# Hybrid encoder kernel: low halves on VectorE, first head's values split out of PSUM, late operands and attention loads placed elsewhere

## The chip, the cores and the metric

The kernel runs on one core of a Trainium2 chip. The metric is device time in microseconds of one launch. Engines are named as in the profile: PE (TensorE) multiplies, DVE (VectorE), ACT (ScalarE) and POOL (GpSimd) work on tiles in on-chip memory (SBUF) and in the accumulator banks (PSUM), SP starts most of the DMA transfers. Every engine runs its instructions in one fixed order and stands still at an instruction whose inputs or whose output's memory isn't ready.

## The reference

Two layers over 1024 tokens of 1024 features, float32 throughout. Layer 0 is a retention mixer with 4 heads (keys of 256, values of 512), layer 1 attends in chunks with 16 heads of 64; each is followed by a squared-ReLU MLP of width 4096.

```python
proj = h @ w_in                                   # retention: q | k | v | g
q = _rope(q, pos);  k = _rope(k, pos) * DK ** -0.5
scores  = einsum(q, k) * intra_decay;  o = scores @ v + (q @ state) * query_decay
o = (o - mean) * rsqrt(var + EPS) * gn_g          # per head
y = (silu(g) * o) @ w_out
...
s = q @ k.T * scale + bias;  p = softmax(s);  y = (p @ v) @ w_out      # attention, band of 576 keys
...
u = relu(h @ w1);  y = (u * u) @ w2               # MLP
x = x + y                                          # after each, with an RMSNorm in front
```

## The kernel before

**Products.** Every large product is three matmuls (`mm3`, L161 to L166): operand and weight are each split into a high half, rounded to TensorE's fast type, and a low half, the rest; high x high, low x high and high x low are summed in PSUM. `split` (L132) makes the halves: the high one as a cast on ACT (L136), the low one as a subtraction on DVE or, where `lo_eng` says "pool", on POOL (L140). So L136 and L140 appear in the profile for many tiles, told apart by their names: vh/vl values of retention, yh/yl its gated output, oh/ol attention's output, whi/wlo weights, ptl transposed probabilities, xl operands of the MLP.

**Stages, by time in the profiled execution.** Projections of q and k with rope (50 to 330 us), of the values (to 440) and of the gate (to 556); retention core, one head after the other (556 to 900); MLP up (to 1240) and down (to 1600); attention's q, k and v (to 1850); attention core (1855 to 2118); MLP up and down again (to the end).

**Values of retention.** `proj_tok` (L451) computes one head's values for 8 token tiles in 8 PSUM banks, and `evac` scales each on ACT and stores it to a DRAM buffer vS. In the core, `issue` (L752) loads q, k and v pieces into a ring of 4 `raw` tiles and `take` (L766) splits them: q and k with DVE, v with ACT and POOL; then it issues the next load, whose ring slot is free when that split has ended. `turn_k` transposes the keys (kth, ktl at L793), `score` (L804) makes the scores, which are masked with maskt (L811) and split (sh, sl). The heads' outputs are normalized by a chain of small operations on tiles of 128x2 (`sm`, L850 to L858, with the square root of L852 on ACT), which ends in `on` (L862, ACT), is transposed by PE (L884), multiplied by the gate (yt, L886) and split (yh, yl).

**Sevens.** Large square products go by seven products of sums instead of eight (`Seven`, L353). `go` runs the products in the order of `steps`: of the first two groups products 1, 2, 5 and 6, then (0,3), (1,3), (0,7), (0,4), (1,7), (1,4), then group by group. `ready` prepares weights two steps ahead: `sums` (L334) adds weight blocks into wS tiles, of which 3 can live at once, and `make` splits them into wh and wl. The operands of products 3, 7 and 4 are made by twelve `late` steps (L301), four for each: t, xh and xl for product 3 (L313), then t3 and its split, then t4 (L319, L320) and its split. `spread` (L426) hangs them behind the products; the scheduler then places them among the rest of each engine's order. The norm's last part (`turn`) hangs behind product 4.

**Attention core.** For each of 16 heads and 4 row groups, `scores` puts q times k into PSUM (pS), DVE adds the bias (bt), writes pr and a row statistic into `sm` (L1144), ACT exponentiates (L1148), DVE inverts the sum (L1149), POOL scales pr (L1150), PE transposes (pt, L1168), ACT and DVE split it (pth, ptl), PE multiplies by the values (po, L1180), ACT and DVE add up osum (L1187, L1188), and osum is split (oh on ACT, ol on POOL). `att_out` multiplies finished heads by the output weights in between; its wlo are on POOL for the heads within the core. `load_q`, `load_k` and `load_b` issue the loads of a head on SP.

Of the kernel before, what the change touches and what calls it, by code (L numbers as in the profile page):

```python
# [9 lines left out]
F32 = mybir.dt.float32  # L10
F32R = mybir.dt.float32r
# [5 lines left out]
P = 128  # L17
S = 1024
# [58 lines left out]
def trunk_kernel(ctx: ExitStack, tc: tile.TileContext, I, out):  # L77
# [246 lines left out]
    class Group:  # L324
# [9 lines left out]
        def sums(self, ws, products):  # L334
            a = self.a
            for p in products:
                self.s[p] = t = ws.tile([P, 4, P], F32, name="wS", tag="wS", bufs=3)
                if p == 5:
                    nc.vector.tensor_tensor(out=t, in0=a[1, 0], in1=a[1, 1], op=ALU.add)
                elif p == 6:  # L340
                    nc.vector.tensor_tensor(out=t, in0=self.s[5], in1=a[0, 0], op=ALU.subtract)
                elif p == 7:
                    nc.vector.tensor_tensor(out=t, in0=a[1, 0], in1=a[0, 0], op=ALU.subtract)
                else:
                    nc.vector.tensor_tensor(out=t, in0=a[0, 1], in1=self.s[6], op=ALU.subtract)
# [80 lines left out]
    def spread(norm, xb, psp, more=()):  # L426

        gen = norm.late(xb)
        hooks = {s: [] for s in range(12)}
        for hf in range(2):  # L430
            hooks[2].append(lambda hf=hf: norm.sums(psp, hf))
            hooks[Seven.NORM].append(lambda hf=hf: norm.turn(psp, hf))
        for i in range(12):
            hooks[1 + (i * 3) // 4].append(lambda: next(gen))
        for s, f in more:
            hooks.setdefault(s, []).append(f)
        return hooks
# [164 lines left out]
    with ExitStack() as ph:  # L602
# [92 lines left out]
        vsc = gp.tile([P, NB, RH], F32, name="vsc")  # L695
        for i in range(RH):
            nc.vector.tensor_tensor(out=vsc[:, :, i], in0=vdec[:, :, i], in1=rcol, op=ALU.mult)
        for hd in range(RH):
            def evac(t, ps, hd=hd):
                vt = tmp_tile(gp, "t")  # L700
                nc.scalar.activation(vt, ps, AF.Copy, scale=vsc[:, t, hd:hd + 1])
                DMA.dma_start(out=vS[hd][t * P:(t + 1) * P, :], in_=vt)
            proj_tok(psp, norm, w_in[:, 2 * D + hd * DV:2 * D + (hd + 1) * DV], evac)

        yp = pool(rs, "yR", RIGHT)
        cq = pool(rq, "coreRqk", RIGHT)
        qk, vv, kt, sc, stt = {}, {}, {}, {}, {}

        def qk_tiles():
            return [cq.tile([P, 2, HT], F32R, name=n, tag=n, bufs=3) for n in ("qkh", "qkl")]  # L710
# [21 lines left out]
    with ExitStack() as ph:  # L732
# [6 lines left out]
        with ExitStack() as st:  # L739
            cp = pool(st, "coreR", RIGHT)  # L740
            pa = pool(st, "psR", None, 8, PSUM)
            maskt = cp.tile([P, RH, P], F32, name="maskt")
            nc.scalar.dma_start(out=maskt, in_=I["mask"])
            fill = Filler()


            items = [(hd, hf, what) for hd in range(RH) for hf in range(2) for what in ("q", "k", "v0", "v1")]
            items = [it for it in items if it not in ((0, 0, "q"), (0, 0, "k"))]
            raws, issued = {}, [0]
            RING = 4  # L750

# [14 lines left out]
            def take(hd, hf, what):  # L766
                if hd == RH:
                    return
                raw = raws[hd, hf, what]
                if what in "qk":  # L770
                    hi, lo = qk[hd, what, hf] = qk_tiles()
                    split(raw, hi, lo)
                else:
                    hi, lo = (cp.tile([P, 2, DV], F32R, name=n, tag=n, bufs=3) for n in ("vh", "vl"))
                    split(raw, hi, lo, "act", "pool")
                    for x in range(2):
                        vv[hd, hf * 4 + 2 * int(what[1]) + x] = (hi[:, x, :], lo[:, x, :])
                if (what, hf) != ("k", 0):
                    issue()
# [96 lines left out]
            def gate(hd, hf, pr, res):  # L876
                ons, gt = res, gtile[hd, hf, pr]
                if pr == 0:
                    ybuf[hd, hf] = tuple(yp.tile([P, 4, HT], F32R, name=n, tag=n, bufs=2) for n in ("yh", "yl"))
                yh, yl = ybuf[hd, hf]  # L880
                for z in range(2):
                    pt = pa.tile([P, 4, P], F32, name="pt", tag="ps")
                    for e in range(4):
                        nc.tensor.transpose(pt[:, e, :], ons[z][:, e * P:(e + 1) * P], ident)  # L884
                    yt = cp.tile([P, 4, P], F32, name="yt", tag="yt", bufs=2)
                    nc.vector.tensor_tensor(out=yt, in0=pt, in1=gt[:, :, z * P:(z + 1) * P], op=ALU.mult)  # L886
                    tsl = slice((2 * pr + z) * P, (2 * pr + z + 1) * P)
                    split(yt, yh[:, :, tsl], yl[:, :, tsl], "act", "pool")
                load_gate()

            for _ in range(RING):
# [4 lines left out]
            for hd in range(RH):  # L896
                if late is not None:
                    fill.gens.append(tail)
                for J in range(4):
                    score(hd, 0, J)  # L900
                take(hd, 0, "v0")
                take(hd, 0, "v1")
                turn_k(hd)
                if late is not None:
                    fill.step(2)
                    gate(*late)
                state(hd, 0)
                state(hd, 1)
                fill.step(4)
                take(hd, 1, "q")  # L910
                take(hd, 1, "k")
                fill.step(3)
                ra = outs(hd, 0, 0)
                fill.step(2)
                rb = outs(hd, 0, 1)
                fill.drain()
                box = dict(psp=pa)
                tail = out_proj(box, hd)
                next(tail)
                gate(hd, 0, 0, ra)  # L920
                for J in range(4):
                    score(hd, 1, J)
                take(hd, 1, "v0")
                take(hd, 1, "v1")
                gate(hd, 0, 1, rb)
                ra = outs(hd, 1, 0)
                if hd + 1 < RH:
                    take(hd + 1, 0, "q")
                rb = outs(hd, 1, 1)
                if hd + 1 < RH:  # L930
                    take(hd + 1, 0, "k")
                gate(hd, 1, 0, ra)
                late = (hd, 1, 1, rb)
# [119 lines left out]
    with ExitStack() as ph:  # L1053
# [9 lines left out]
            DMA.dma_start(out=T[hd, "q"].bitcast(F32), in_=qA[hd // 2][hd % 2].rearrange("z f c -> (z f) c"))  # L1063

        def load_k(hd):
            t = cq.tile([P, 2, S], F32R, name="kk", tag="kk", bufs=2)
            src = kA[hd // 2][hd % 2]
            for z in range(2):
                DMA.dma_start(out=t[z * DH:(z + 1) * DH].bitcast(F32), in_=src)
# [9 lines left out]
            nc.gpsimd.memset(bt[DH:P, 0:DH], -NEG)  # L1079
            T[hd, "b"] = bt  # L1080

        for hd in range(2):
            load_q(hd)
            load_k(hd)
            load_b(hd)

        obuf = {}

# [4 lines left out]
        with ExitStack() as st:  # L1093
# [77 lines left out]
            def values(hd, g):  # L1171
# [16 lines left out]
                nc.vector.tensor_tensor(out=osum[mine, :], in0=po[mine, :], in1=osum[mine, :], op=ALU.add)  # L1188
                sl = slice(g * 2 * P, (g + 1) * 2 * P)
                oh, ol = obuf[p]  # L1190
                split(osum[mine, :], oh[mine, sl], ol[mine, sl], "act", "pool")

            units = [(hd, g) for hd in range(AH) for g in (0, 2, 1, 3)]
            n = len(units)
# [4 lines left out]
            for i in range(n + L2):  # L1199
# [8 lines left out]
                if i >= L2:  # L1208
                    values(*units[i - L2])
                    j = i - L2 + 1  # L1210
                    if j in (16, 32):
                        fill.add(att_out(dict(psp=pF), j // 8 - 2, 2, "pool"))
                if L1 <= i < n + L1:
                    turn(*units[i - L1], 2)
                fill.step(1)
# [96 lines left out]
```

## Time and profile before

| | us |
|---|---|
| median of 3 runs | 2859.15 (2856.14 to 2859.59) |
| profiled execution, its own time | 2858.98 |
| its span | 2857.2 |
| PE busy | 2763.7 (97%) |
| DVE busy | 1624.3 (57%) |
| ACT busy | 1080.7 (38%) |
| POOL busy | 305.1 (11%) |

The span is one execution as the hardware profiler saw it; the own time of that execution is 1.8 us longer. PE is busy nearly all the time, so the views that count are those that show where it waits, at which clock it runs, and what ends its waits. The mean granted clock is 0.985 of full speed; a share of 0.50 in a stretch is the lower of the clock's two levels, 1.2 of 2.4 GHz.

### The profile page before, as it was taken

The numbers are of one execution on the slowest core, as the hardware profiler recorded it, in microseconds if no ns is written. First come the engines' busy times: TensorE is split into PE (matmuls) and PEld (weight loads), VectorE is DVE, ScalarE is ACT, GpSimd is POOL, SyncE is SP. The second block draws the span as 40 slices with busy tenths as digits, with TensorE's granted clock in tenths as the row PEclk, the third lists the DMA queues.
The fourth block names the chain that finished last, engine by engine and source line by source line (L and its number), as shares of the span: only waits on it lengthen the run. The fifth ranks groups of instructions, "written<-read, shape, count | busy, mean of one in ns | idle before, by whom it ended". The sixth has DMA issues, their size and how long they took to land.

```text
span 2857.2 us, 34484 instructions
## 1 busy us (share of the span) xinstructions
PE 2763.7 (97%) x12762; PEld 2272.0 (80%) x12762; DVE 1624.3 (57%) x2851; ACT 1080.7 (38%) x1932; POOL 305.1 (11%) x351
## 2 busy tenths in 40 slices
PE   8999999989999999999999899989999999999998
PEld 7888888768877788878888778769877888788887
DVE  5431123366557766654545877678878666544545
ACT  4001221243225544432213534478875444422222
POOL 1320000042111000000000000255540000000000
PEclk9999999989999999999999999999999999999999
DMA  4322333342211332343322265685621333433321
GB/s 142 107 91 78 107 114 99 114 155 93 84 52 37 103 111 100 115 141 106 108 77 85 55 201 153 166 211 143 169 71 51 116 115 111 140 100 103 111 85 59
DMA packets 247770, 313.02 MB, mean 110 GB/s; under 512 B 14665, under 2 KB 172465, under 8 KB 245553
## 3 DMA queue, kind: packets, MB, share of 16 engines
q1 hardware_dynamic: 245792, 306.30, 34.8%
q0 software_dynamic: 1536, 4.20, 0.5%
q8 instruction: 100, 1.64, 0.3%
q14 instruction: 70, 0.57, 0.1%
q10 hardware_dynamic: 272, 0.32, 0.0%
HBM read 222.64 MB, written 90.74 MB: 110 GB/s over the span
## 4 chain that ended last, share of the span: by engine, by line
PE 86%; DVE 6%; ACT 4%; issue 2%; DMA 1%; POOL 0%; SPq 0%; POOLq 0%; DVEq 0%; ACTq 0%
PE ps L165 18%; PE ps L164 18%; PE ps L166 18%; PE pA L164 6%; PE pA L166 5%; PE pA L165 5%; PE pC L164 3%; PE pC L166 3%; PE pC L165 3%; PE pB L164 1%; PE pB L166 1%; PE pB L165 1%; PE po L1180 1%; PE pt L1168 1%; ACT pr L1148 1%
## 5 line engine op out<-in xcount | busy, mean ns | idle before, releaser
L491 DVE TENSOR_TENSOR h<-ps,h 128x512 f32<-128x512 f32 x352 | 242.2, 689 | 343.3 <-PE ps L166 342.3
L136 ACT CAST whi<-wraw 128x1024 fp32r<-128x1024 f32 x132 | 139.0, 1053 | 765.2 <-PE ps L165 580.6
L165 PE MATMUL ps<-ul,whi 128*128 128x512 f32 x960 | 374.0, 390 | 1.8 <-DVE ul L140 1.8
L166 PE MATMUL ps<-uh,wlo 128*128 128x512 f32 x960 | 373.5, 389 | 0.0
L164 PE MATMUL ps<-uh,whi 128*128 128x512 f32 x960 | 373.1, 389 | 0.0
L164 PE MATMUL pA<-xh,wh 128*128 128x512 f32 x704 | 279.1, 401 | 12.3 <-ACT wh L136 9.3
L166 PE MATMUL pA<-xh,wl 128*128 128x512 f32 x704 | 277.4, 395 | 8.5 <-DVE wl L140 8.5
L165 PE MATMUL pA<-xl,wh 128*128 128x512 f32 x704 | 278.4, 395 | 0.0
L140 DVE TENSOR_TENSOR wlo<-wraw,whi 128x1024 fp32r<-128x1024 f32 x127 | 160.1, 1260 | 173.1 <-ACT whi L136 173.0
L165 PEld LDWEIGHTS ps<-ul,whi 128*128 128x128 f32 x960 | 180.2, 188 | 41.1 <-DVE ul L140 3.6
L164 PEld LDWEIGHTS ps<-uh,whi 128*128 128x128 f32 x960 | 180.0, 188 | 38.1 <-ACT uh L136 0.9
L166 PEld LDWEIGHTS ps<-uh,wlo 128*128 128x128 f32 x960 | 180.2, 188 | 37.1
L164 PE MATMUL ps<-hhi,whi 128*128 128x512 f32 x512 | 202.8, 396 | 2.3 <-ACT whi L136 1.5
L165 PE MATMUL ps<-hlo,whi 128*128 128x512 f32 x512 | 202.3, 395 | 0.0
L166 PE MATMUL ps<-hhi,wlo 128*128 128x512 f32 x512 | 202.3, 395 | 0.0
L164 PEld LDWEIGHTS pA<-xh,wh 128*128 128x128 f32 x704 | 134.3, 191 | 51.8 <-DVE c L417 13.4
L166 PEld LDWEIGHTS pA<-xh,wl 128*128 128x128 f32 x704 | 133.6, 190 | 38.9 <-DVE wl L140 10.1
L165 PEld LDWEIGHTS pA<-xl,wh 128*128 128x128 f32 x704 | 134.2, 191 | 27.4
L136 ACT CAST wh<-wS 128x512 fp32r<-128x512 f32 x176 | 109.1, 621 | 120.4 <-PE pB L165 57.4
L164 PE MATMUL pC<-xh,wh 128*128 128x512 f32 x352 | 139.8, 397 | 2.3 <-ACT wh L136 2.3
L166 PE MATMUL pC<-xh,wl 128*128 128x512 f32 x352 | 140.4, 399 | 0.6 <-DVE wl L140 0.6
L140 DVE TENSOR_TENSOR wl<-wS,wh 128x512 fp32r<-128x512 f32 x176 | 120.9, 687 | 33.6 <-ACT wh L136 33.0
(229 smaller groups left out, 5660.4 us busy)
## 6 DMA issues: line engine op xcount, KB each, us to landing
wr<-in_mlp_w_dram SPq DMA_DIRECT2D x32, 1024.0 KB, 5.5
uD<-c SPq DMA_DIRECT2D x128, 256.0 KB, 2.0
wraw<-in_mlp_w_dram SPq DMA_DIRECT2D x64, 512.0 KB, 3.5
xr<-uD SPq DMA_DIRECT2D x128, 256.0 KB, 3.1
wraw<-in_ret_w_in_dram SPq DMA_DIRECT2D x48, 512.0 KB, 4.1
kk<-kA SPq DMA_DIRECT2D x32, 512.0 KB, 8.4
wr<-in_att_w_in_dram SPq DMA_DIRECT2D x12, 1024.0 KB, 5.2
vS<-t SPq DMA_DIRECT2D x32, 256.0 KB, 2.0
```

Of the source, the lines that this page charges most:

```text
L136: nc.scalar.copy(out=hi, in_=src)
L140: eng.tensor_tensor(out=lo, in0=src, in1=hi.bitcast(F32), op=ALU.subtract)
L164: nc.tensor.matmul(ps, lhsT=lh, rhs=rh, start=start, stop=False, skip_group_check=more)
L165: nc.tensor.matmul(ps, lhsT=lh, rhs=rl, start=False, stop=False, skip_group_check=more)
L166: nc.tensor.matmul(ps, lhsT=ll, rhs=rh, start=False, stop=stop, skip_group_check=more)
L491: nc.vector.tensor_tensor(out=hv, in0=ps, in1=hv, op=ALU.add)
L1148: nc.scalar.activation(pr[:, :w], pr[:, :w], AF.Exp, bias=sm[:, 0:1], scale=-1.0, accum_out=sm[:, 1:2])
L1168: nc.tensor.transpose(pt[:, c - done:c - done + P], pr[:, (kb - k0) * P:(kb - k0 + 1) * P], ident)
L1180: nc.tensor.matmul(po[:, oc:oc + n], lhsT=T[hd, "v"][:, kb, :], rhs=t[:, off[kb]:off[kb] + n], start=i == 0, stop=i == len(seq) - 1)
```

## The change

Six edits. (1) `sums` may hold four wS tiles. (2) The twelve `late` steps hang behind products 0, 0, 1, 1, 2, 3, 4, 4, 5, 6, 7, 8 in place of 1, 1, 2, 3, 4, 4, 5, 6, 7, 7, 8, 9. (3) The first half of head 0's values (t < 4) is split straight from PSUM in `evac`, the high half by ACT, the low half by one operation of DVE, into tiles that the pool yR offers for retention's output later; those pieces are no longer stored, loaded or taken. (4) The mask is loaded by SP into a pool opened earlier, not by ACT's queue at the core's start. (5) The low halves vl (14 left, 128x1024), yl (32, 128x512), ol (64, 64x256) and the core's four wlo (128x1024) are made by DVE, not POOL. (6) The keys of even and odd heads have a tile of their own each, and the loads before attention go out as k0, q0, q1, b0, k1, b1; the first key tile thereby gets the memory that q's tile had before, and q's the keys'.

```diff
--- before.py
+++ after.py
@@ -334,7 +334,7 @@
         def sums(self, ws, products):
             a = self.a
             for p in products:
-                self.s[p] = t = ws.tile([P, 4, P], F32, name="wS", tag="wS", bufs=3)
+                self.s[p] = t = ws.tile([P, 4, P], F32, name="wS", tag="wS", bufs=4)
                 if p == 5:
                     nc.vector.tensor_tensor(out=t, in0=a[1, 0], in1=a[1, 1], op=ALU.add)
                 elif p == 6:
@@ -431,7 +431,7 @@
             hooks[2].append(lambda hf=hf: norm.sums(psp, hf))
             hooks[Seven.NORM].append(lambda hf=hf: norm.turn(psp, hf))
         for i in range(12):
-            hooks[1 + (i * 3) // 4].append(lambda: next(gen))
+            hooks[(0, 0, 1, 1, 2, 3, 4, 4, 5, 6, 7, 8)[i]].append(lambda: next(gen))
         for s, f in more:
             hooks.setdefault(s, []).append(f)
         return hooks
@@ -695,16 +695,26 @@
         vsc = gp.tile([P, NB, RH], F32, name="vsc")
         for i in range(RH):
             nc.vector.tensor_tensor(out=vsc[:, :, i], in0=vdec[:, :, i], in1=rcol, op=ALU.mult)
+        yp = pool(rs, "yR", RIGHT)
+        vv = {}
+        v0 = [yp.tile([P, 4, HT], F32R, name=n, tag=n, bufs=2) for n in ("yh", "yl")]
         for hd in range(RH):
             def evac(t, ps, hd=hd):
+                if hd == 0 and t < 4:
+                    hi, lo = vv[0, t] = tuple(z[:, t, :] for z in v0)
+                    sc = vsc[:, t, 0:1]
+                    nc.scalar.activation(hi, ps, AF.Copy, scale=sc)
+                    nc.vector.scalar_tensor_tensor(out=lo, in0=ps, scalar=sc, in1=hi.bitcast(F32), op0=ALU.mult, op1=ALU.subtract)
+                    return
                 vt = tmp_tile(gp, "t")
                 nc.scalar.activation(vt, ps, AF.Copy, scale=vsc[:, t, hd:hd + 1])
                 DMA.dma_start(out=vS[hd][t * P:(t + 1) * P, :], in_=vt)
             proj_tok(psp, norm, w_in[:, 2 * D + hd * DV:2 * D + (hd + 1) * DV], evac)
 
-        yp = pool(rs, "yR", RIGHT)
         cq = pool(rq, "coreRqk", RIGHT)
-        qk, vv, kt, sc, stt = {}, {}, {}, {}, {}
+        qk, kt, sc, stt = {}, {}, {}, {}
+        maskt = cq.tile([P, RH, P], F32, name="maskt")
+        DMA.dma_start(out=maskt, in_=I["mask"])
 
         def qk_tiles():
             return [cq.tile([P, 2, HT], F32R, name=n, tag=n, bufs=3) for n in ("qkh", "qkl")]
@@ -739,13 +749,11 @@
         with ExitStack() as st:
             cp = pool(st, "coreR", RIGHT)
             pa = pool(st, "psR", None, 8, PSUM)
-            maskt = cp.tile([P, RH, P], F32, name="maskt")
-            nc.scalar.dma_start(out=maskt, in_=I["mask"])
             fill = Filler()
 
 
             items = [(hd, hf, what) for hd in range(RH) for hf in range(2) for what in ("q", "k", "v0", "v1")]
-            items = [it for it in items if it not in ((0, 0, "q"), (0, 0, "k"))]
+            items = [it for it in items if it[:2] != (0, 0)]
             raws, issued = {}, [0]
             RING = 4
 
@@ -772,7 +780,7 @@
                     split(raw, hi, lo)
                 else:
                     hi, lo = (cp.tile([P, 2, DV], F32R, name=n, tag=n, bufs=3) for n in ("vh", "vl"))
-                    split(raw, hi, lo, "act", "pool")
+                    split(raw, hi, lo)
                     for x in range(2):
                         vv[hd, hf * 4 + 2 * int(what[1]) + x] = (hi[:, x, :], lo[:, x, :])
                 if (what, hf) != ("k", 0):
@@ -885,7 +893,7 @@
                     yt = cp.tile([P, 4, P], F32, name="yt", tag="yt", bufs=2)
                     nc.vector.tensor_tensor(out=yt, in0=pt, in1=gt[:, :, z * P:(z + 1) * P], op=ALU.mult)
                     tsl = slice((2 * pr + z) * P, (2 * pr + z + 1) * P)
-                    split(yt, yh[:, :, tsl], yl[:, :, tsl], "act", "pool")
+                    split(yt, yh[:, :, tsl], yl[:, :, tsl])
                 load_gate()
 
             for _ in range(RING):
@@ -898,8 +906,9 @@
                     fill.gens.append(tail)
                 for J in range(4):
                     score(hd, 0, J)
-                take(hd, 0, "v0")
-                take(hd, 0, "v1")
+                if hd:
+                    take(hd, 0, "v0")
+                    take(hd, 0, "v1")
                 turn_k(hd)
                 if late is not None:
                     fill.step(2)
@@ -1063,7 +1072,7 @@
             DMA.dma_start(out=T[hd, "q"].bitcast(F32), in_=qA[hd // 2][hd % 2].rearrange("z f c -> (z f) c"))
 
         def load_k(hd):
-            t = cq.tile([P, 2, S], F32R, name="kk", tag="kk", bufs=2)
+            t = cq.tile([P, 2, S], F32R, name="kk", tag=f"kk{hd % 2}", bufs=1)
             src = kA[hd // 2][hd % 2]
             for z in range(2):
                 DMA.dma_start(out=t[z * DH:(z + 1) * DH].bitcast(F32), in_=src)
@@ -1079,10 +1088,8 @@
             nc.gpsimd.memset(bt[DH:P, 0:DH], -NEG)
             T[hd, "b"] = bt
 
-        for hd in range(2):
-            load_q(hd)
-            load_k(hd)
-            load_b(hd)
+        for f, hd in ((load_k, 0), (load_q, 0), (load_q, 1), (load_b, 0), (load_k, 1), (load_b, 1)):
+            f(hd)
 
         obuf = {}
 
@@ -1188,7 +1195,7 @@
                 nc.vector.tensor_tensor(out=osum[mine, :], in0=po[mine, :], in1=osum[mine, :], op=ALU.add)
                 sl = slice(g * 2 * P, (g + 1) * 2 * P)
                 oh, ol = obuf[p]
-                split(osum[mine, :], oh[mine, sl], ol[mine, sl], "act", "pool")
+                split(osum[mine, :], oh[mine, sl], ol[mine, sl])
 
             units = [(hd, g) for hd in range(AH) for g in (0, 2, 1, 3)]
             n = len(units)
@@ -1209,7 +1216,7 @@
                     values(*units[i - L2])
                     j = i - L2 + 1
                     if j in (16, 32):
-                        fill.add(att_out(dict(psp=pF), j // 8 - 2, 2, "pool"))
+                        fill.add(att_out(dict(psp=pF), j // 8 - 2, 2))
                 if L1 <= i < n + L1:
                     turn(*units[i - L1], 2)
                 fill.step(1)
```

On DVE in the first Seven, at the change from the weights of products 1, 2, 5 and 6 to those of 3, 7 and 4 (wl and wS are weights, t and xl operands, c results). Before, the sum wS(1,7) of L343 and its wl stand late:

```order
L319 SCALAR_TENSOR_TENSOR t_6844<-h_86,gall,xh_6219 128x512
L140 TENSOR_TENSOR xl_6609<-t_6821,xh_6608 128x512
L320 TENSOR_TENSOR t_6844<-t_6844,xl_6220 128x512
L535 SCALAR_TENSOR_TENSOR c<-c,rB 128x512
L343 TENSOR_TENSOR wS<-wr 128x512
L140 TENSOR_TENSOR xl_6609<-t_6844,xh_6608 128x512
L140 TENSOR_TENSOR wl<-wr,wh 128x512
L417 TENSOR_TENSOR c<-pC,s_6814 128x512
L319 SCALAR_TENSOR_TENSOR t_6872<-h_88,gall,xh_6219 128x512
L535 SCALAR_TENSOR_TENSOR c<-c,rB 128x512
L320 TENSOR_TENSOR t_6872<-t_6872,xl_6220 128x512
L140 TENSOR_TENSOR wl<-wS,wh 128x512
```

With the change the first late operands and both sums of L343 stand ahead of the first L535:

```order
L140 TENSOR_TENSOR wl<-wS,wh 128x512
L140 TENSOR_TENSOR xl_6574<-t_6650,xh_6573 128x512
L345 TENSOR_TENSOR wS<-wr,wS 128x512
L313 SCALAR_TENSOR_TENSOR t_6674<-h_83,gall,b_6673 128x512
L343 TENSOR_TENSOR wS<-wr 128x512
L140 TENSOR_TENSOR wl<-wS,wh 128x512
L140 TENSOR_TENSOR xl_6574<-t_6674,xh_6573 128x512
L343 TENSOR_TENSOR wS<-wr 128x512
L535 SCALAR_TENSOR_TENSOR c<-c,rB 128x512
L313 SCALAR_TENSOR_TENSOR t_6725<-h_85,gall,b_6724 128x512
```

Two steps of t and xl and the wS sum have moved ahead of L535, and the wl of that last sum follows as row 702, 27 rows behind that L535; before, the wl (last row above) was row 660 and the L535 ahead of the late operands row 629.

On SP, at the end of attention's projections (wraw are output weights, skew the bias). Before:

```order
L147 DMA wraw<-in_att_w_out_dram 128x2x512 x3
L1063 DMA qh<-qA_9064 128x1024
L1069 DMA kk<-kA_9072 64x2048 x2
L1076 DMA bt<-skew_9081 64x576 x2
L1063 DMA qh<-qA_9064 128x1024
L1069 DMA kk<-kA_9072 64x2048 x2
L1076 DMA bt<-skew_9082 64x576 x2
```

With the change:

```order
L147 DMA wraw<-in_att_w_out_dram 128x2x512 x4
L1078 DMA kk<-kA_9058 64x2048 x2
L1072 DMA qh<-qA_9050 128x1024 x2
L1085 DMA bt<-skew_9067 64x576 x2
L1078 DMA kk<-kA_9058 64x2048 x2
L1085 DMA bt<-skew_9068 64x576 x2
```

The keys of head 0 go ahead of both q loads, and one more wraw goes ahead of the keys.

On DVE in the attention core, around one unit. Before:

```order
L1188 TENSOR_TENSOR osum<-po,osum 64x256
L140 TENSOR_TENSOR ptl<-pt,pth 128x256
L1149 RECIPROCAL sm<-sm 128x1
L491 TENSOR_TENSOR h_84<-ps,h_84 128x512
L1144 ISA pr,sm<-pS,bt 128x384
L1144 ISA sm 128x1
L140 TENSOR_TENSOR ptl<-pt,pth 128x384
L1144 ISA pr,sm<-pS,bt 128x512
L1144 ISA sm 128x1
```

With the change (L1151, L1156 and L1195 are the former L1144, L1149 and L1188):

```order
L1195 TENSOR_TENSOR osum<-po,osum 64x256
L140 TENSOR_TENSOR ptl<-pt,pth 128x256
L491 TENSOR_TENSOR h_84<-ps,h_84 128x512
L1156 RECIPROCAL sm<-sm 128x1
L140 TENSOR_TENSOR ol<-osum,oh 64x256
L1151 ISA pr,sm<-pS,bt 128x384
L1151 ISA sm 128x1
L140 TENSOR_TENSOR ptl<-pt,pth 128x384
L1151 ISA pr,sm<-pS,bt 128x512
L1151 ISA sm 128x1
```

The new subtraction ol stands behind the reciprocal and ahead of the next score tile's operation.

## Rows read from the trace of the kernel before

**Rows 1.** PE's waits: line and releaser: us in total, times, longest.

```profile
PE ps L164 <- DVE sl L140: 10.8, 3, 4.0
PE pS L1139 <- DMA kk<-kA: 9.3, 1, 9.3
PE pA L164 <- ACT wh L136: 9.3, 3, 4.1
PE pA L166 <- DVE wl L140: 8.5, 3, 2.9
PE ps L164 <- ACT vh L136: 6.3, 1, 6.3
PE pt L884 <- ACT on L862: 5.8, 3, 4.3
```

**Rows 2.** Stretches: us, busy us (instructions) by engine, granted clock PEclk, DMA.

```profile
571.00:581.20 10.20, 6.87 (x14) 4.49 (x15) 6.54 (x6) 4.69 (x8) 5.67 (x2) 0.50 0.79 262
598.30:605.10 6.80, 4.68 (x15) 4.08 (x16) 5.69 (x14) 4.96 (x9) 1.79 (x2) 0.50 0.36 125
625.60:629.00 3.40, 3.38 (x8) 2.71 (x9) 3.28 (x10) 3.40 (x7) 0.00 (x0) 0.50 0.91 285
963.50:970.30 6.80, 4.04 (x10) 3.00 (x10) 5.99 (x10) 1.85 (x3) 0.00 (x0) 0.50 0.70 219
```

**Rows 3.** Timeline 591 to 625, DVE and POOL: start, duration, engine, line, operation.

```profile
591.77 1.39 DVE L850 TENSOR_TENSOR sm<-mv,odec 128x2 f32<-128x2 f32 x1
593.69 1.85 DVE L851 TENSOR_SCALAR sm<-sm 128x2 f32<-128x2 f32 x1
596.42 1.21 DVE L855 TENSOR_TENSOR sm<-sm 128x2 f32<-128x2 f32 x1
597.67 1.18 DVE L856 SCALAR_TENSOR_TENSOR sm<-sm 128x2 f32<-128x2 f32 x1
622.34 2.34 POOL L140 TENSOR_TENSOR vl<-raw,vh 128x1024 fp32r<-128x1024 f32 x1 [0.70 <-ACT vh L136]
622.60 2.10 DVE L854 SCALAR_TENSOR_TENSOR sm<-sm 128x2 f32<-128x2 f32 x1
624.82 0.14 DVE L855 TENSOR_TENSOR sm<-sm 128x2 f32<-128x2 f32 x1
```

**Rows 4.** Timeline of ACT, 568 and 621; in brackets idle time and releaser.

```profile
568.86 0.59 ACT L793 CAST ktl<-pt 128x512 fp32r<-128x512 f32 x1 [3.08 <-DMA gS<-t]
621.22 1.04 ACT L136 CAST vh<-raw 128x1024 fp32r<-128x1024 f32 x1 [2.50 <-DMA raw<-vS]
```

**Rows 5.** Timeline of DVE and PE in the first Seven.

```profile
961.51 0.69 DVE L343 TENSOR_TENSOR wS<-wr 128x512 f32<-128x512 f32 x1
965.78 0.69 DVE L140 TENSOR_TENSOR wl<-wS,wh 128x512 fp32r<-128x512 f32 x1
966.52 0.79 PE L166 MATMUL pA<-xh,wl 128*128 128x512 f32 x1 [2.76 <-DVE wl L140]
```

**Rows 6.** Timeline of SP's queue at the start of the attention core.

```profile
1855.03 1.33 SPq L1069 DMA_DIRECT2D kk<-kA  x2
```

**Rows 7.** Attention core: two stretches, groups of 1885:2115 (busy, mean ns | idle), timeline at 2031.

```profile
1885.00:2025.00 140.00, 135.52 (x929) 121.49 (x928) 121.45 (x348) 117.61 (x293) 78.57 (x127) 1.00 0.65 165
2025.00:2115.00 90.00, 84.06 (x584) 74.54 (x581) 79.34 (x226) 78.85 (x194) 50.49 (x78) 1.00 0.48 123
...
L1188 DVE TENSOR_TENSOR osum<-po,osum 64x256 f32<-64x256 f32 x59 | 24.8, 420 | 4.5 <-ACT osum L1187 3.6
L1150 POOL TENSOR_SCALAR pr<-pr,sm 128x640 f32<-128x640 f32 x58 | 46.3, 799 | 48.9 <-DVE sm L1149 30.0 <-PE pt L1168 13.2 <-PE pS L1140 4.4
L140 POOL TENSOR_TENSOR ol<-osum,oh 64x256 fp32r<-64x256 f32 x60 | 43.9, 731 | 34.9 <-ACT oh L136 26.8 <-DVE sm L1149 5.4 <-DMA vst<-vA 1.5
...
2031.73 1.21 DVE L140 TENSOR_TENSOR wlo<-wraw,whi 128x1024 fp32r<-128x1024 f32 x1
2032.01 2.05 POOL L1150 TENSOR_SCALAR pr<-pr,sm 128x384 f32<-128x384 f32 x2 [0.90 <-DVE sm L1149]
```

## The prediction

> **What bounds the kernel now.** The kernel is limited by PE, so I read first where PE stands still and then where it runs slowly. The view of PE's waits says the first [rows 1]: 9.3 us for kk (start of the attention core), three waits for sl, 10.8 together (start of a retention head), three pairs for wh and wl, 9.3 and 8.5 together (start of each Seven), 6.3 for vh (first retention head) and 5.8 for on (tails of retention heads). The table by stretches says the second [rows 2]: the granted clock is 0.50 (1.2 GHz) in short stretches right behind those waits. Such a stretch costs half of PE's busy time in it: 6.87/2 = 3.4 us from 571, 4.68/2 = 2.3 from 598.3, 3.38/2 = 1.7 from 625.6 (behind the first sl wait; the two others look alike), 4.04/2 = 2.0 from 963.5 (first Seven). So a wait is worth itself and a part of the slow stretch behind it. The sum is made against the profiled execution, 2858.98 us (span 2857.2), which is the median of the runs (2859.15) to 0.2 us.
>
> **Head 0 of the retention core.** PE waits 6.3 us for vh. The cause stands on ACT: its cast of ktl waits 3.08 us for a store, gS, whose source shares memory with it, and the vh casts queue behind [rows 4]. After the change the first four value tiles of head 0 are split out of PSUM during the V projection, and their store, load and later split fall away; the mask comes in early through SP; kth and ktl lie elsewhere, so ACT has no store to wait for. The four added subtractions (128x512, the nearest row is wl's 0.69 us [rows 5], so 2.8) I cost at nothing: a token tile's bank is complete while the products of the tiles behind it still run, and those hide them; without that cover they cost 2.8.
>
> The waits for on, 5.8, end a chain of tiny DVE operations. There the rows show what busy shares hide. L855 on 128x2 takes 0.14 us at 624.82, but L850, L851, L855 and L856 take 1.39, 1.85, 1.21 and 1.18 us between 591 and 599, and L854 takes 2.10 us from 622.60 to 624.70: POOL's vl, begun at 622.34 for 2.34 us, ends there [rows 3]. A DVE operation on tiles in SBUF stands still while POOL subtracts. With vl and yl off POOL, the chain behind head 0 loses 1.39 + 1.85 + 1.21 + 1.18 - 4 x 0.15 = 5.0 us, more than the longest on wait. Of 6.3 + 5.8 = 12.1 us I leave 1.3: 10.8 gained, and 5 of the 3.4 + 2.3 of the slow stretches. **15.8 us.**
>
> The page "SBUF — State Buffer" of the Trainium skill (Terms, shared port pair) calls the port pair of DVE and GpSimd an exclusive lock that is held for a full instruction; the 2.10 us row agrees.
>
> **Head boundaries, three times.** PE waits for sl, 3.6 us each [rows 1], because it needs a PSUM bank that the first sl has still to read. On the way to that sl lie two things. ACT's vh is held 2.50 us by the load of raw, with the square root and the sh casts behind it [rows 4]; raw's slot is freed by a vl, which on DVE takes 1.21 us (as wlo, same shape [rows 7]) and not 2.34, so raw lands some 1.1 us earlier. And L854's 2.10 us, of which 1.9 are POOL's [rows 3], go. That is 3.0; I take 2.8 each, 8.4, and the slow stretches behind, 3 x 1.7 = 5.1. **13.5 us.** Against it, 14 vl at 1.21 and 32 yl at 0.69 put 39 us on DVE over the 340 us of this core. PE waits for DVE there at the chains above and hardly elsewhere; I charge **1.5 back** (bounds 0 and 5). The smaller waits at the last head's end I count at nothing.
>
> **The Sevens, three times.** In the first, wS(1,7) is summed only at 961.51 and its wl comes at 965.78, both late in a DVE run almost without a gap; PE restarts at 966.52 [rows 5]. What the change does is read from the order: two t and two xl of the late operands and the sum wS move ahead of the norm's last steps, into time in which DVE waits for ACT. From the first L535 behind them to that wl stood 31 rows, now 27, and a row takes 0.6 to 0.7 us (the wS has 0.69). So wl comes 2.5 us earlier, and wh is no longer late. The bounds are 0 (the scheduler gives the place away again) and (9.3 + 8.5)/3 = 5.9. I take 2.7 each, 8, and half of a slow stretch like the first (1.0) each, 3. **11 us.**
>
> **Attention's start.** kk leaves SP at 1855.03 [rows 6], when the last but one product frees its memory, and PE waits 9.3 us. The new place of kk is free long before, but on SP it now stands behind a fourth wraw, whose slot waits for the second wlo on DVE, which lies among the last tiles of the projection; so it leaves a little before 1855, how much I can't read. qh takes the old place and leaves at 1855: then one load of 0.5 MB is left behind the last product where two halves of kk, 1 MB, were. At half the time that gives 9.3/2 = 4.6; if qh shares the DMA engines with kk all the way, 0. I take **3**.
>
> **Attention's steady part, the cost.** In 1885 to 2115 DVE is busy 121.45 + 79.34 = 200.8 of 230 us, and PE 219.6 [rows 7]. 60 of the 64 ol and two wlo fall into it. An ol on POOL takes 0.73; on DVE the nearest row is osum of the same shape, 0.42: 60 x 0.42 = 25.2, and 2 x 1.21 = 2.4 [rows 7]. DVE is then asked for 228.4 of 230 us. If none of its 29.2 idle us must stay, the cost is 0; if all, 27.6. The idle time is mostly waiting for ACT in a fixed order, and a later DVE finds ACT further on, so I let a quarter stay, 7.3: **6 us back** (228.4 + 7.3 - 230). Freeing POOL gives PE nothing there: no wait of PE for pr stands among the large ones [rows 1].
>
> The sum: 15.8 + 13.5 - 1.5 + 11 + 3 - 6 = 35.8, so 2858.98 - 35.8 = **2823 us**.
>
> **Rivals.** (a) *ol is held by POOL's pr, in part.* POOL goes on scaling pr, 0.80 us for 128x640, each started by a reciprocal, and in DVE's new order a reciprocal stands right before most ol. The trace has only the other direction: beside wlo, on DVE from 2031.73 for 1.21 us, POOL's two pr of 128x384 took 2.05 us together, longer than two of 128x640 [rows 7]. If ol is held for half a pr, 0.4 us x 60 = 24 come on top and no idle time is left: 228.4 + 24 - 230 = 22 instead of 6, so 2839. For it speaks that row; against it, that ol may start before POOL does. The Trainium skill's "GPSIMD Engine Reference" (1. Specifications, SBUF interfaces) names contention with DVE instructions that have two SBUF inputs, which ol is and the other DVE work of that stretch is not. By that, (a) is what happens. (b) *Slower.* The same in full: every ol waits out a whole pr (60 x 0.8 = 48) and half of the old idle time stays (14.6): 228.4 + 48 + 14.6 - 230 = 61 instead of 6, so 2878. It decides from the point where the stretch grows by 42 us, which with that idle time is 0.48 us of holding for each ol. Against it: ACT's oh, for which ol waits as well, spreads their starts. (c) *The late operands give nothing*, since wl still ends the chain and the moved rows only push others: 11 us less, 2834. (d) *The clock does not come back*: shorter waits still leave 0.50 behind them; 5 + 5.1 + 3 = 13 less, 2836. (e) *Better*: DVE's idle time in attention is all usable (6), the Sevens lose most of their waits (another 8), and the small waits that I counted at nothing go too (some 5): 2804.
>
> **How the numbers follow.** Forecast 2823 (2813 to 2832): 0.45. (a) 0.18, (b) 0.06, (c) 0.10, (d) 0.08, (e) 0.11, two of (a), (c) and (d) together and so near the old time 0.02. The range leaves out (b), the ends of (e) and the joint cases: 2801 to 2849. About 0.2% (5.7 us) is what a measurement of this kernel can tell from no change: faster by more than that 0.90, within it 0.04, slower 0.06.
>
> **What would show it.** Right: PE's waits for vh and on under 1.5 us together in head 0, for sl under 1 each; no 128x2 operation of DVE over 0.3 us in the retention core; one wait of about 3 us in each Seven; about 6 at attention's start; and the clock at 1.00 where a head begins. Wrong: a mean of ol on DVE well over 0.42, or the stretch from 1885 to 2115 longer by more than 10 us, would put the error into attention; waits gone without the gain would put it into the clock.

## The result, and the profile after

| | before | after |
|---|---|---|
| median, us | 2857.64 (2855.34 to 2859.59, 4 runs) | 2835.38 (2834.74 to 2836.27, 4 runs) |
| span of the profiled execution | 2857.2 | 2833.9 |
| mean granted clock | 0.985 | 0.990 |

The ratio is 0.9923, 95% interval 0.9905 to 0.9940: about 22 us faster. The forecast was 2823, range 2801 to 2849; of the 36 us forecast 13 did not come.

Where the time went, by the start or end of the same matmuls in both traces:

| stretch | before, us | after, us | difference | forecast |
|---|---|---|---|---|
| start to the first product of the first Seven (pA) | 924.1 | 895.7 | -28.4 | -27.8 |
| first Seven, MLP up | 321.8 | 318.2 | -3.6 | -3.7 |
| Seven of attention's projections | 258.3 | 253.9 | -4.4 | -3.7 |
| wait for the first score matmul (pS) | 9.3 | 11.7 | +2.4 | -3 |
| first pS to last po | 255.5 | 269.1 | +13.6 | +6 |
| Seven, MLP up of layer 1 | 324.3 | 321.6 | -2.7 | -3.7 |

These rows sum to -23.1 of the 23.3 us between the spans. Everything ahead of attention came near the sum; both terms of attention missed. The last row can't be put down to the change: the kernel with vl and yl alone (first experiment), whose Sevens are those of the kernel before, has 320.8 there.

PE's waits after (line and releaser: us in total, times, longest):

```profile
PE pt L1175 <- DVE ptl L140: 14.1, 27, 1.3
PE pS L1146 <- DMA qh<-qA: 11.7, 1, 11.7
PE pA L166 <- DVE wl L140: 10.0, 4, 3.4
PE pS L1146 <- DVE sm L1151: 7.1, 10, 3.2
PE pt L892 <- ACT on L870: 5.1, 1, 5.1
...
PE ps L164 <- ACT yh L136: 1.7, 1, 1.7
...
PE ps L164 <- DVE sl L140: 0.6, 3, 0.2
```

Beside [rows 1]: the waits for vh and those of pA for wh are gone, and those for sl fell from 10.8 us to 0.6. In the attention core PE waits for ptl 27 times where it waited 10 times before:

```profile
PE pt L1168 <- DVE ptl L140: 5.8, 10, 1.2
```

A wait of 11.7 us stands where 9.3 was. The waits for wl did not shrink. The waits for on are one of 5.1 us where they were three, 5.8 together; it stands at head 0's first pair of tiles, where PE had waited 0.5 us before.

The retention core by stretches, and its first head boundary (length, busy us of PE, weight load, DVE, ACT, POOL, then the granted clock):

```profile
556.00:645.00 89.00, 83.68 (x406) 70.01 (x405) 59.50 (x128) 38.67 (x62) 0.00 (x0) 0.96 0.48 160
645.00:730.00 85.00, 84.80 (x406) 70.64 (x405) 54.28 (x119) 29.90 (x47) 0.00 (x0) 1.00 0.31 99
730.00:815.00 85.00, 84.79 (x405) 70.55 (x404) 53.13 (x114) 27.47 (x43) 0.00 (x0) 1.00 0.24 75
815.00:900.00 85.00, 83.31 (x388) 68.98 (x388) 66.07 (x127) 42.29 (x69) 0.00 (x0) 1.00 0.12 38
...
609.00:614.00 5.00, 4.79 (x26) 3.88 (x25) 5.00 (x15) 4.04 (x8) 0.00 (x0) 1.00 0.58 214
```

POOL does nothing there any more, DVE does more, and the clock is 1.00 where a head begins (609 to 614, and from 645 on); at 625.6, the first such place in the trace before, it was 0.50 [rows 2]. The 0.96 of the first stretch belongs to the wait for on within head 0. The operations on 128x2 tiles (min/median/max ns):

```profile
L859 DVE TENSOR_SCALAR sm<-sm x16: 136/169/170, 579.8 to 851.1; 128x2 f32<-128x2 f32 x16
L862 DVE SCALAR_TENSOR_TENSOR sm<-sm x16: 129/160/161, 582.3 to 851.9; 128x2 f32<-128x2 f32 x16
```

L862 is the former L854 that took 2.10 us [rows 3]; its longest is now 161 ns.

### The profile page after: what moved, and what is told of

It is laid out like the page before. It is cut to its first block, busy times and chain, and to the rows that moved or that the text cites. A ratio compares the mean times of both kernels' runs of the same rounds, so it can differ in the third digit from the quotient of the medians.

```text
span 2833.9 us, 34421 instructions
## 1 busy us (share of the span) xinstructions
PE 2751.2 (97%) x12762; PEld 2262.3 (80%) x12762; DVE 1655.6 (58%) x2969; ACT 1080.2 (38%) x1930; POOL 170.2 (6%) x235
## 4 chain that ended last, share of the span: by engine, by line
PE 85%; DVE 8%; ACT 3%; DMA 2%; issue 1%; SPq 0%; POOL 0%; DVEq 0%; ACTq 0%
PE ps L166 18%; PE ps L164 18%; PE ps L165 18%; PE pA L164 6%; PE pA L166 5%; PE pA L165 5%; PE pC L164 3%; PE pC L166 3%; PE pC L165 3%; DVE pr L1151 1%; DVE ptl L140 1%; PE pB L164 1%; PE pB L166 1%; PE pB L165 1%; PE po L1187 1%
## 5 line engine op out<-in xcount | busy, mean ns | idle before, releaser
L491 DVE TENSOR_TENSOR h<-ps,h 128x512 f32<-128x512 f32 x352 | 242.4, 689 | 339.4 <-PE ps L166 338.9
L164 PEld LDWEIGHTS pA<-xh,wh 128*128 128x128 f32 x704 | 133.4, 190 | 43.2 <-DVE c L417 13.6
L165 PE MATMUL pC<-xl,wh 128*128 128x512 f32 x352 | 138.6, 394 | 0.0
```

Source lines behind the costliest of these rows:

```text
L164: nc.tensor.matmul(ps, lhsT=lh, rhs=rh, start=start, stop=False, skip_group_check=more)
L165: nc.tensor.matmul(ps, lhsT=lh, rhs=rl, start=False, stop=False, skip_group_check=more)
L491: nc.vector.tensor_tensor(out=hv, in0=ps, in1=hv, op=ALU.add)
```

## Experiments

**vl and yl alone, on the kernel before.**

```diff
-                    split(raw, hi, lo, "act", "pool")
+                    split(raw, hi, lo)
...
-                    split(yt, yh[:, :, tsl], yl[:, :, tsl], "act", "pool")
+                    split(yt, yh[:, :, tsl], yl[:, :, tsl])
```

> The kernel before with nothing changed but vl and yl of the retention core on DVE. Theory (POOL's subtractions hold up DVE's small operations): no 128x2 operation above 0.3 us, the three waits for sl fall from 10.8 to under 4 us, the clock at the head boundaries is 1.00, the wait for vh stays at 6; 12 to 18 us faster than before, 2839 to 2845. Rival (the head boundaries were late because of the loads of raw, and what the whole change gained in the core came from head 0's values): sl waits above 7 us, less than 8 us gained.

Measured: 2834.59 us, ratio 0.9924 (0.9907 to 0.9940). Two lines give as much as the whole change, more than was expected of them. PE's waits (us in total, times, longest):

```profile
PE ps L164 <- ACT vh L136: 6.2, 1, 6.2
PE pt L884 <- ACT on L862: 4.3, 1, 4.3
PE pA L164 <- ACT wh L136: 9.3, 3, 4.1
```

The waits for sl are down to 0.8 us, and the clock of the stretches 645 to 900 is 1.00 as in the changed kernel. vh (6.2) and wh (9.3) stand as before, as they should with nothing done about them. The first pA comes at 902.5, so the core is 21.6 us shorter; the difference to 28.4, 6.8, is left for head 0's values and the mask. Two things went together here: no 128x2 operation lasts over 0.17 us any more, and ACT's vh no longer waits for raw, 6.3 us in three waits at the head boundaries before. How much each gave was not tested.

**The same question from the other side: the changed kernel with vl and yl on POOL.**

```diff
-                    split(raw, hi, lo)
+                    split(raw, hi, lo, "act", "pool")
...
-                    split(yt, yh[:, :, tsl], yl[:, :, tsl])
+                    split(yt, yh[:, :, tsl], yl[:, :, tsl], "act", "pool")
```

> The changed kernel with vl and yl back on POOL: the same question from the other side. Theory: the sl waits and the slow clock at the three head boundaries come back, 12 to 18 us slower than the changed kernel, 2847 to 2853. Rival: under 8 us slower.

Measured: 2860.02 us, ratio to the kernel before 1.0015 (1.0006 to 1.0025), 25 us above the changed kernel: more than expected, and not faster than before at all (1.7 to 7.1 us slower by the interval). The 128x2 operations and PE's waits:

```profile
L859 DVE TENSOR_SCALAR sm<-sm x16: 169/171/2376, 580.3 to 866.1; 128x2 f32<-128x2 f32 x16
L862 DVE SCALAR_TENSOR_TENSOR sm<-sm x16: 160/162/2208, 581.4 to 867.8; 128x2 f32<-128x2 f32 x16
```

```profile
PE ps L164 <- DVE sl L140: 9.8, 3, 3.3
PE pt L892 <- ACT on L870: 6.0, 3, 3.2
```

The same instructions as above, with a median that is unchanged and a longest of 2.2 to 2.4 us, the length of a POOL subtraction; and the sl waits are back, 9.8 us. The first pA comes at 914.9, 19.2 us later than in the changed kernel. What vl and yl on POOL cost is so shown from both sides: 22 and 25 us of the whole time, 21.6 and 19.2 of it in the core. (The first experiment moved 16 vl, this one 14, as head 0's first half has none here.) By this side 9.2 us are left for head 0's values and the mask. All the other edits together are worth nothing: the first pA is 9.2 us earlier than in the kernel before, and from the first pS to the last po it takes 270.4 us, 14.9 longer.

**The late operands alone, on the kernel before.**

```diff
-                self.s[p] = t = ws.tile([P, 4, P], F32, name="wS", tag="wS", bufs=3)
+                self.s[p] = t = ws.tile([P, 4, P], F32, name="wS", tag="wS", bufs=4)
...
-            hooks[1 + (i * 3) // 4].append(lambda: next(gen))
+            hooks[(0, 0, 1, 1, 2, 3, 4, 4, 5, 6, 7, 8)[i]].append(lambda: next(gen))
```

> The kernel before with nothing changed but the fourth wS tile and the earlier hooks of the late operands. Theory: the waits for wh in the Sevens go (9.3 to about 1), those for wl stay at 8 to 10; 9 to 13 us faster, 2844 to 2848. Rival (the gain between the core and attention came along with another part): less than 4 us.

Measured: 2850.64 us, ratio 0.9977 (0.9968 to 0.9987): 5.6 us by the medians, 3.7 to 9.1 by the interval, 8.9 by the spans of the two profiled executions. The direction is the theory's, the size below it.

```profile
PE pA L166 <- DVE wl L140: 9.5, 3, 3.4
PE ps L164 <- DVE sl L140: 10.9, 3, 4.1
```

The row for wh, 9.3 us in three waits, is gone; wl stays at 9.5, as expected. In the changed kernel the three Sevens are 10.7 us shorter by the traces, 8.0 without the third. PE's wait moved from two places to one, and DVE's run before wl is what ends it.

**ol on POOL in the changed kernel, and no ol at all.** The second kernel leaves out the 64 subtractions and sets the low halves to zero once.

```diff
-                split(osum[mine, :], oh[mine, sl], ol[mine, sl])
+                split(osum[mine, :], oh[mine, sl], ol[mine, sl], "act", "pool")
```

> The changed kernel with the 64 attention subtractions ol back on POOL. Theory (DVE has no room): the time from the first score matmul to the last po matmul falls from 269.1 to 256 to 259 us, PE's waits for ptl from 14.1 to about 6, and the whole from 2835 to 2822 to 2825. Rival (what was lost there is the late start, or the shared port that holds POOL's pr): under 4 us come back, 2831 to 2836.

> The changed kernel without the 64 subtractions ol: the low halves of attention's output are set to zero once, so that part of the computation is left out. If ol on POOL costs nothing, this runs attention in the same time as ol on POOL, within 2 us (256 to 259 from first score to last po). If ol on POOL costs time too, by holding the port against DVE or by delaying pr on POOL, this one is 4 us or more faster than that.

Measured: 2822.92 us with ol on POOL (ratio to before 0.9879, 0.9864 to 0.9893), 2823.02 us without ol (0.9885, 0.9870 to 0.9901). From the first score matmul to the last po it takes 257.4 and 259.4 us, against 269.1 in the changed kernel. PE's waits with ol on POOL:

```profile
PE pS L1146 <- DMA qh<-qA: 10.4, 1, 10.4
PE pt L1175 <- DVE ptl L140: 6.2, 11, 1.2
```

The waits for ptl fall from 14.1 to 6.2 (before: 5.8). ol on POOL costs nothing that shows, and on DVE about 12 us. The rival that the late start made the loss falls: 12 us came back by ol alone. The port is not decided by these runs, since without ol on DVE nothing of ol holds POOL's pr either. PE's own waits for pr speak against it, in the kernel before, the changed one and the one with ol on POOL:

```profile
PE pt L1168 <- POOL pr L1150: 0.7, 3, 0.2
PE pt L1175 <- POOL pr L1157: 1.0, 1, 1.0
PE pt L1175 <- POOL pr L1157: 1.8, 4, 1.1
```

**Why ol costs that on DVE: the dose.** Each ol twice on DVE, and ol on DVE for every second row group only.

```diff
+                nc.vector.tensor_tensor(out=ol[mine, sl], in0=osum[mine, :], in1=oh[mine, sl].bitcast(F32), op=ALU.subtract)
```

> The changed kernel with each of the 64 subtractions ol done twice on DVE (the same result both times). If attention's core is limited by DVE's work, the second one costs its whole time, 64 x 0.42 = 27 us less the remaining idle time: 20 to 27 us above 2835, 2855 to 2862, more than the 12 that the first one cost. If the first one cost its place in the order (a wait for oh each time) and not DVE's time, the second one, which waits for nothing, costs less than 12.

```diff
-                split(osum[mine, :], oh[mine, sl], ol[mine, sl])
+                split(osum[mine, :], oh[mine, sl], ol[mine, sl], "act", "pool" if g % 2 else "dve")
```

> The changed kernel with ol on DVE for every second row group and on POOL for the others. If the cost sets in where DVE runs out of idle time, half of the work costs much less than half of 12 us: 2823 to 2827. If each ol costs the same, 2828 to 2830.

Measured: 2856.76 us with twice the work (ratio 1.0001, 0.9991 to 1.0010: the whole gain is gone) and 2828.11 with half (0.9899, 0.9884 to 0.9914), at the lower end of what was expected if each ol costs the same. The lengths from the first pS to the last po:

| ol on DVE | length, us | each further ol costs |
|---|---|---|
| 0 (all on POOL) | 257.4 | |
| 32 | 261.7 | 4.3/32 = 0.13 |
| 64 (the change) | 269.1 | 7.4/32 = 0.23 |
| 128 | 288.3 | 19.2/64 = 0.30 |

The operation lasts 0.42 to 0.47 us. Kernels that do the same work here differ by some us, 255.5 to 257.4 with ol on POOL and 266.6 to 270.4 with 64 on DVE, so 0.13 and 0.23 can't be told apart. The first 64 cost 0.14 to 0.23 us each by these ends, the last 64 clearly more, 0.28 to 0.34. So it is DVE's time that runs out, gradually. The last 64 wait for nothing of ACT and cost most, so it isn't the wait for oh. There is no sharp point at which the cost sets in: half of the work cost 5.2 us in the whole time, above the 2823 to 2827 that the free idle time would have allowed and near the even share, 6.2. DVE's groups with ol twice (busy, mean ns | idle before):

```profile
L1199 DVE TENSOR_TENSOR ol<-osum,oh 64x256 fp32r<-64x256 f32 x55 | 25.8, 469 | 0.8
L140 DVE TENSOR_TENSOR ol<-osum,oh 64x256 fp32r<-64x256 f32 x54 | 22.6, 419 | 1.3
L1156 DVE RECIPROCAL sm<-sm 128x1 f32<-128x1 f32 x107 | 16.3, 152 | 1.4 <-ACT pr L1155 0.9
```

In the kernel before, over as long a stretch:

```profile
L1149 DVE RECIPROCAL sm<-sm 128x1 f32<-128x1 f32 x116 | 18.6, 160 | 14.7 <-ACT pr L1148 12.5
```

The idle time in front of the reciprocals, 14.7 us there and 6.0 in the changed kernel, is down to 1.4: there the idle time is nearly used up.

With half of ol on DVE, PE's waits for ptl lie between the two:

```profile
PE pt L1175 <- DVE ptl L140: 11.4, 22, 1.1
```

**Attention's start.** The old order of loads and the old tags; both undone together with ol; and ol and the core's wlo on POOL with the new and with the old loads.

```diff
-        for f, hd in ((load_k, 0), (load_q, 0), (load_q, 1), (load_b, 0), (load_k, 1), (load_b, 1)):
-            f(hd)
+        for hd in range(2):
+            load_q(hd)
+            load_k(hd)
+            load_b(hd)
```

> The changed kernel with the loads before attention in the old order (q, k, bias head by head) and one tag with two buffers for the keys. Theory A (the order and places of kk and qh make PE wait 11.7 in place of 9.3 us): the wait falls to 9.5 or less, the whole to 2832 to 2833. Theory B (the fourth wraw, 0.5 MB more in front of them, and the writes of kA that now fall into the same time, make it): the wait stays at 11 to 13, the whole within 2 us of 2835.

> Both together. If the two act apart from each other the gains add: 2820 to 2823 by theory A on the loads, 2822 to 2825 by theory B.

```diff
-                        fill.add(att_out(dict(psp=pF), j // 8 - 2, 2))
+                        fill.add(att_out(dict(psp=pF), j // 8 - 2, 2, "pool"))
```

> The changed kernel with ol and the attention core's four wlo back on POOL, so that three wraw and not four go ahead of the first keys on SP. Theory B (the fourth wraw delays kk and qh): PE's wait at attention's start falls from 10.4 us (ol alone on POOL) to 7 to 9, the whole from 2822.9 to 2820 to 2821.5. Rival (the writes of kA that share the DMA engines make it): the wait stays above 10, the whole within 1.5 us of 2822.9.

> As e4 (ol and the core's wlo on POOL, so three wraw in front), but with the loads in the old order and the old key tags. It tells the order of the loads apart from the wraw. If the new order is worth something once the fourth wraw is out of the way, PE's wait at attention's start is longer here than the 8.0 us there, 9 to 11, and the whole 1 to 3 us above it; if not, both are within 1 us.

| kernel | loads | wraw ahead of them | ol | PE's wait, us | time, us (ratio to before) |
|---|---|---|---|---|---|
| the change | new | 4 | DVE | 11.7 | 2835.38 (0.9923) |
| old loads | old | 4 | DVE | 11.0 | 2833.17 (0.9917) |
| ol on POOL | new | 4 | POOL | 10.4 | 2822.92 (0.9879) |
| both | old | 4 | POOL | 10.6 | 2823.17 (0.9885) |
| core on POOL | new | 3 | POOL | 8.0 | 2825.02 (0.9886) |
| core on POOL, old loads | old | 3 | POOL | 8.3 | 2822.24 (0.9877) |

SP's queue (start, from the first issue to the last) in the changed kernel, and with three wraw:

```profile
1799.66 16.54 SPq L147 DMA_DIRECT2D wraw<-in_att_w_out_dram  x4
1816.24 1.22 SPq L1078 DMA_DIRECT2D kk<-kA  x2
1817.87 1.10 SPq L1072 DMA_DIRECT2D qh<-qA  x2
```

```profile
1800.59 13.21 SPq L147 DMA_DIRECT2D wraw<-in_att_w_out_dram  x3
1813.93 1.12 SPq L1078 DMA_DIRECT2D kk<-kA  x2
1818.86 1.10 SPq L1072 DMA_DIRECT2D qh<-qA  x2
```

In both, kk is issued right behind the last wraw. With four, the last goes out just ahead of it, by 1816.20, and it, kk and both q (2.5 MB) are under way at once; qh, issued at 1817.87, is what PE starts on at 1829.53. With three, kk leaves 4.9 us ahead of qh. So theory B holds for the wait: the fourth wraw is worth 2.3 to 2.4 us of it (10.4 to 8.0, 10.6 to 8.3), the order of the loads 0.2 to 0.7, with no steady sign. The rival that the writes of kA make it falls, since the wait didn't stay above 10. Six kernels with the same new start wait 10.4 to 11.7 us, so the order's share can't be told from no effect. In the whole time it doesn't show: the last four kernels lie within 2.8 us, with intervals that overlap. Four kernels (ol on POOL, both, and core on POOL with either loads) are faster than both the kernel before and the changed one, at 0.988 of before; among them the runs don't decide.

## Why the prediction was right and where it missed

**Head 0 and the head boundaries: right in the sum, 27.8 forecast, 28.4 measured.** How it divides is less certain. The step on POOL's subtractions was the main one: in my sum 13.5 for the boundaries, some 4 of waits and 2.3 of clock for on at head 0, less the 1.5 charged for DVE, so about 18; measured, 21.6 from one side and 19.2 from the other. For head 0's values I had about 9.5, 6.3 of wait and the rest clock; 6.8 and 9.2 are left for them. That the sum agrees to 0.6 us is in part luck, for one step of it failed: I let the waits for on go with POOL's hold, and the recorded sign was under 1.5 us for vh and on together in head 0. The old wait for on, 4.3 us at the second pair of tiles, did go, but one of 5.1 came at the first pair. PE is done with its products at 579.00, before the first 128x2 operation of that pair's chain (L858, 579.60). DVE's operation that the square root waits for, and ACT, in the changed kernel:

```profile
579.81 0.14 DVE L859 TENSOR_SCALAR sm<-sm 128x2 f32<-128x2 f32 x1
...
579.25 1.04 ACT L136 CAST qkh<-raw 128x1024 fp32r<-128x1024 f32 x1 [3.21 <-DMA raw<-qS]
580.32 1.28 ACT L860 ACT_TABLE_LOAD   x1
581.61 0.20 ACT L860 ACTIVATE sm<-sm 128x2 f32<-128x2 f32 x1
...
583.27 1.45 ACT L870 ACTIVATE on<-ps,sm 128x512 f32<-128x512 f32 x2 [0.29 <-DVE sm L866]
```

PE waits from 579.00 to 584.10 for the on of 583.27. Ahead of it ACT's qkh waits 3.21 us for a load of raw, then come that cast and 1.28 us for a table, and the square root of the chain stands behind all three. Its input is there at 579.95 and it starts at 581.61, so this place on ACT explains 1.7 of the 5.1 us; the rest is the chain itself, on a DVE that does a vl just ahead of it (577.81, 1.19 us) and a qkl within it (580.33, 1.23 us). That is read from this one place; it was not tested by an experiment of its own. The clock is at 0.65 on the mean of 584 to 590, so this wait has its slow stretch too.

**The clock came back** with the waits, at the three head boundaries, as said; rival (d) falls.

**The Sevens: the mechanism right, the size less than 11 as far as the runs tell.** wh went, wl stayed, one wait of about 3 us in each. The traces give 10.7, of which the third Seven's 2.7 came without these edits too; the late operands alone gave 5.6, and their interval, 3.7 to 9.1, leaves 11 out. Rival (c), no gain at all, falls.

**Attention's start: the wrong sign.** Forecast 3 us less wait, measured 2.4 more. The failing step is "one load of 0.5 MB is left behind the last product where two halves of kk were". I counted the loads behind the last product and not all that shares the DMA engines with them: kk did not leave early enough to be done, since the fourth wraw stood in front of it, and qh landed behind all three. The order had shown the wraw; I gave it no bytes. My lower bound of 0 let qh share the DMA engines with kk alone, and so was too high.

**Attention's steady part: right mechanism, half the size.** Forecast 6, measured 13.6, beyond the 10 us that the prediction named as the sign of an error here; 1.3 of them lie before the first po. The demand on DVE was near: 27.6 us more by the sum, and 24.6 more from the first pS to the last po (217.8 busy before, 242.4 after). The mis-sized term is the idle time that must stay, 7.3 us (a quarter). After:

```profile
1850.00:1990.00 140.00, 129.49 (x893) 116.57 (x891) 130.87 (x370) 113.90 (x283) 51.15 (x83) 1.00 0.58 151
1990.00:2080.00 90.00, 82.05 (x545) 73.64 (x545) 82.77 (x235) 72.77 (x180) 33.56 (x54) 0.96 0.54 140
```

DVE is busy 130.87 + 82.77 = 213.6 of 230 us, so 16.4 us of idle stay in as long a stretch, more than half of the 29.2 [rows 7], while PE is already waiting: PE is down from 219.6 to 211.5. Here PE and DVE, busy 92% and 93% of this stretch, wait for each other before either is full. The clock, 0.96 in the second stretch where it was 1.00, means some 7 us at the lower level and so about 3 us of time, which I had at nothing.

**Rival (a), ol held by POOL's pr: not what happened.** Groups of 1850 to 2090 (busy, mean ns | idle before):

```profile
L140 DVE TENSOR_TENSOR ol<-osum,oh 64x256 fp32r<-64x256 f32 x59 | 26.8, 454 | 2.8 <-ACT oh L136 1.1
L1156 DVE RECIPROCAL sm<-sm 128x1 f32<-128x1 f32 x116 | 18.1, 156 | 6.0 <-ACT pr L1155 5.5
L1157 POOL TENSOR_SCALAR pr<-pr,sm 128x640 f32<-128x640 f32 x57 | 48.0, 842 | 96.6 <-DVE sm L1156 55.1 <-PE pS L1147 23.0 <-PE pt L1175 7.3
L1157 POOL TENSOR_SCALAR pr<-pr,sm 128x384 f32<-128x384 f32 x15 | 12.1, 809 | 15.3 <-DVE sm L1156 11.4 <-PE pS L1147 4.0
```

ol takes 454 ns on the mean, 0.03 above osum: held in a few places, about 60 x 0.03 = 2 us. It is pr on POOL that grew, from 799 to 842 ns for 128x640: ol begins first, right behind the reciprocal that also starts pr, and POOL waits. With ol on POOL the 128x640 take 803 ns. The 128x384 grew from 691 to 809, but that is the work of wlo: with ol on POOL and wlo on DVE they take 799, with both on POOL 692. The row that spoke for the rival showed just that direction. By the "GPSIMD Engine Reference" of the Trainium skill (1. Specifications, SBUF interfaces) there is contention, and there is; which of the two waits isn't told by that, and here it was POOL's pr, for which PE waits only 1.0 us in all. **Rival (b)** falls with it.

**Rival (e)** is not what came either, and without the loss in attention the change would have come near the forecast: with ol on POOL 2822.9. That this meets the 2823 of the forecast is chance, since the forecast has a cost of 6 us in attention and a gain of 3 at its start.

## What to carry to other kernels

Read small operations one by one: a busy share hides an operation of 0.16 us that takes 2, and moving the work beside it that makes it last so long (here two lines) was worth more than all the placing of loads and operands. Before moving work to an engine, ask for its idle time in that stage and don't count on all of it: here, with PE just as full, more than half couldn't be used. The same move was worth 22 us in one stage and cost 12 in the next. Count every transfer that is under way together with the one that is waited for, not just those that follow the event.

## What the runs showed of the hardware that was not expected

Some DVE operations with all their inputs in SBUF and POOL's operations hold each other up, in both directions. In the retention core of the kernel before, 128x2 operations of 0.17 us lasted up to 2.33 us beside POOL's subtractions, one with a single tensor as its input (L851) among them. But the reciprocals on the same tile were not held (one of 0.17 us at 622.40 ran beside the vl begun at 622.34, which held L854 [rows 3]), nor the 116 in the attention core, in which POOL was busy 129.1 of 230 us:

```profile
L851 DVE TENSOR_SCALAR sm<-sm x16: 169/170/2329, 587.8 to 875.1; 128x2 f32<-128x2 f32 x16
L853 DVE RECIPROCAL sm<-sm x16: 131/166/167, 588.7 to 876.6; 128x2 f32<-128x2 f32 x16
L1149 DVE RECIPROCAL sm<-sm x116: 144/164/166, 1886.5 to 2113.0; 128x1 f32<-128x1 f32 x116
```

In the other direction, POOL's scaling of 128x384 went from a mean of 691 to 809 ns with wlo on DVE, and that of 128x640 from 799 to 842 with ol there. DVE operations that read PSUM were not stretched: ptl of 128x512 took 687 ns on the mean before, with 60 subtractions and 116 scalings on POOL in the same stretch, and 682 after.
